# Turning the rows of h for the gates: two 16-bit planes through the DMA crossbar in place of TensorE

## The chip, the cores and the metric

The kernel runs on one core of one Trainium2 chip. The metric is the device time of one execution in microseconds. The engines are named as the profile names them: PE (TensorE's matmuls), PEld (its weight loads), DVE (VectorE), ACT (ScalarE), POOL (GpSimd) and SP (SyncE, which issues every DMA of this kernel on one queue).

## The reference

Two layers over 512 tokens of width 1024. A layer mixes tokens (layer 0 by a neighbourhood attention, layer 1 by a latent attention), adds the result to its input, and then adds a gated embedding. The part that matters here is what stands behind the mixer:

```python
for i in range(DEPTH):
    xn = rmsnorm(x, norm_g[i])
    ...
    h = x + y
    gate = jax.nn.sigmoid(rmsnorm(h, ple_norm[i]) @ ple_w_gate[i])
    x = h + gate * (p[i] @ ple_w_proj[i])
return rmsnorm(x, final_norm)
```

All arrays are 32-bit floats. `y` is the gated output of the mixer times `w_out`.

## The kernel before, in words

A matrix product in full precision is made of three products in a reduced 32-bit format: each operand is split into a high part (ScalarE copies it into that format) and a low part (what is left, by VectorE or GpSimd), and high x high, low x high and high x low are summed in PSUM. So each weight that arrives from memory as `wraw` is split into `whi` (line 77, ScalarE) and `wlo` (line 78, GpSimd), with three buffers of `wraw`; the load of a weight waits until GpSimd has freed the buffer of three loads before.

A layer's second part runs in two stages, for 4 blocks of 128 tokens (t) and 2 halves of 512 columns (n).

- `out_proj` (line 375) multiplies the mixer's output by `w_out`, 24 matmuls for each of the 8 results, and adds each to the rows of the residual in SBUF (`r`, line 387). After each result it calls `turn_h` (line 789).
- `turn_h` multiplies the 128 x 512 piece by the norm's gain (`hg`, line 792, VectorE), turns it into columns, four blocks of 128 x 128, and splits it into the high and the low part of `hnT` (lines 84 and 86, ScalarE and VectorE). `hnT[t]` has 8 column blocks of the high part and 8 of the low; half n fills four of each. A piece is one (t, n); a layer has eight. With n = 1 it also sums the squares of the rows.
- `gate_phase` (line 425) multiplies `hnT[t]` by the gate's weights, again 24 matmuls for each of 8 results (`ps_mm`, two PSUM buffers). A result's matmuls go by weight chunk c = 0 to 3; chunks 0 and 1 use the half n = 0 of `hnT[t]`, chunks 2 and 3 the half n = 1. Then come the sigmoid (line 440, ScalarE), the product with the embedding's projection (line 441) and the add (line 443). In layer 0 the finished rows are normed, turned (`x1n`) and feed the next layer; in layer 1 they are normed and stored.

Turning is done by `transposes` (line 119): four TensorE transposes against an identity into one PSUM tile, `ps_T`, from which both splits read. The same helper turns other rows too, which the change doesn't touch.

Tiles come from pools that hand out buffers in turn: `hg` has three, `ps_T` three, and the pool `zp` (tag "z") eight of 128 x 512, which hold the mixer's gates z and are free by the time of `out_proj`. The order of the instructions on each engine is fixed when the kernel is built, by a scheduler; on the chip each engine takes its instructions in that order, and SyncE's DMAs are issued in the order of its queue.

Of the kernel before, what the change touches and what calls it, by code (L numbers as in the profile page):

```python
# [12 lines left out]

F32 = mybir.dt.float32
F32R = mybir.dt.float32r
AF = mybir.ActivationFunctionType
ALU = mybir.AluOpType
AX = mybir.AxisListType
PSUM = bass.MemoryType.PSUM
P = 128  # L20
S = 512
# [18 lines left out]
class Trunk:  # L40
# [19 lines left out]
    def bigtile(self, name):  # L60
        return self.big.tile([P, 4, S], F32R, name=name, tag="big")

# [5 lines left out]
    def load_w(self, ap, n, extra=False, parts=1, rest=None):  # L68
        nc = self.nc
        pool = self.wx if extra else self.wp  # L70
        raw = self.wp.tile([P, 1024], F32, name="wraw", tag="wraw", bufs=3)
        hi = pool.tile([P, n if extra else 1024], F32R, name="whi", tag="whi", bufs=self.wxn if extra else 3)
        lo = pool.tile([P, n if extra else 1024], F32R, name="wlo", tag="wlo", bufs=self.wxn if extra else 3)
        w = n // parts
        for c in [slice(i * w, (i + 1) * w) for i in range(parts)]:
            nc.sync.dma_start(raw[:, c], ap[:, c])
            nc.scalar.activation(hi[:, c], raw[:, c], AF.Copy)  # L77
            (rest or nc.gpsimd).tensor_tensor(out=lo[:, c], in0=raw[:, c], in1=hi[:, c].bitcast(F32), op=ALU.subtract)  # L78
# [3 lines left out]
    def split(self, hi, lo, src, scale=1.0):  # L82
        nc = self.nc
        self.last_copy = nc.scalar.activation(hi, src, AF.Copy, scale=scale)  # L84
        if scale == 1.0:
# [15 lines left out]
    def inv_rms(self, scratch, src, n):  # L101
        nc = self.nc
        ss = self.small.tile([P, 1], F32, name="ss", tag="ss")
        rs = self.small.tile([P, 1], F32, name="rs", tag="rs")
        nc.scalar.activation(scratch, src, AF.Square, accum_out=ss)
        nc.vector.tensor_scalar(ss, ss, 1.0 / n, EPS, op0=ALU.mult, op1=ALU.add)  # L106
# [19 lines left out]
    def rows_to_cols(self, xn, dst):  # L126

        for g in range(2):
            t = self.transposes([xn[:, (4 * g + i) * P:(4 * g + i + 1) * P] for i in range(4)])
            hi, lo = dst(g)  # L130
            self.split(hi, lo, t.rearrange("p (a b) -> p a b", a=4))


    @staticmethod
    def terms(w, xT, ks):
# [12 lines left out]
    def z_phase(self, wap, xT, js, after=None, R=None, ws=None):  # L148
# [5 lines left out]
        def finish(j, ps):  # L154
            z = zs[j] = self.zp.tile([P, S], F32, name="z", tag="z")
            with self.tc.issue_after(after) if after is not None else nullcontext():
                if R is None:
                    nc.scalar.activation(z, ps, AF.Silu)
                else:
                    nc.vector.tensor_tensor(out=z, in0=ps, in1=R, op=ALU.mult)  # L160
                    nc.scalar.activation(z, z, AF.Silu)

# [23 lines left out]
    def half_of(self, u, O, e):  # L186
        main, rest = (slice(0, 64), slice(64, 128))[::1 - 2 * e]
        self.nc.scalar.activation(u[main], O[rest], AF.Copy)  # L188
        self.nc.vector.tensor_tensor(out=u[main], in0=O[main], in1=u[main], op=ALU.add)  # L189
# [18 lines left out]
    def na_heads(self, pool, xT, zs, oT):  # L208
# [5 lines left out]
        def project(j):  # L214
            if j % 2 == 0:
# [3 lines left out]
                for kt in range(4):  # L219
# [5 lines left out]
                    self.mms(ps[:, :256], t)  # L225
                    vt = pool.tile([P, S], F32R, name="vt", tag="vt", bufs=8)
                    self.v_split(vt, ps[:, :256])
# [3 lines left out]
            self.proj_T(psq, wq, xT)  # L231
            sa = pool.tile([P, S], F32R, name="sa", tag="qs", bufs=4)
            sb = pool.tile([P, S], F32R, name="sb", tag="qs", bufs=4)
            nc.scalar.activation(sa[0:64], psq[0:64], AF.Copy, scale=0.125)
# [482 lines left out]
    def run(self):  # L717
        tc, nc, a = self.tc, self.nc, self.a
# [6 lines left out]
        with tc.tile_pool(name="pre", bufs=4, reuse_waits="tile") as pool:  # L725
            warm = pool.tile([P, S], F32R, name="warm", bufs=1)
            nc.vector.memset(warm.bitcast(F32), 1.0)
            ps = self.psum("T")
# [33 lines left out]
            turned = self.transposes([ss[:, t:t + 1].to_broadcast([P, P]) for t in range(NT)])  # L762
# [14 lines left out]
        for layer in range(2):  # L777
            with tc.tile_pool(name=f"out{layer}", bufs=4, reuse_waits="tile") as pool:
# [10 lines left out]
                def turn_h(t, n):  # L789

                    hg = pool.tile([P, S], F32, name="hg", tag="hg", bufs=3)
                    nc.vector.tensor_tensor(out=hg, in0=res[t][:, n * S:(n + 1) * S],
                                            in1=gp[:, n * S:(n + 1) * S], op=ALU.mult)
                    if n == 0:
                        hnT[t] = self.big.tile([P, 2 * KD, P], F32R, name="hnT", tag="big")
                    ps = self.transposes([hg[:, i * P:(i + 1) * P] for i in range(4)])
                    self.split(hnT[t][:, 4 * n:4 * n + 4, :], hnT[t][:, KD + 4 * n:KD + 4 * n + 4, :],
                               ps.rearrange("p (a b) -> p a b", a=4))
                    if n == 1:
                        sq = pool.tile([P, D], F32, name="sq", tag="xn", bufs=2)  # L800
                        rh[t] = self.inv_rms(sq, res[t], D)

                self.out_proj(a["na_o"] if layer == 0 else a["mla_o"], oT, res, turn_h, last)
                if layer == 0:
                    x1T = ([self.bigtile(f"x1h{g}") for g in range(2)], [self.bigtile(f"x1l{g}") for g in range(2)])
# [143 lines left out]
```

## Time and profile before

| | |
|---|---|
| runs of the kernel | 672.23, 672.34, 673.18 us (median 672.34) |
| the profiled execution, first to last instruction (span) | 670.9 us |
| TensorE matmul busy | 659.2 us (98%) |
| VectorE, ScalarE, GpSimd busy | 367.9 (55%), 408.2 (61%), 396.2 us (59%) |
| granted TensorE clock, mean | 0.998 |

The profiled execution's own time is its span and what lies around it, which the profile doesn't show; the span is 1.4 us under the median of the runs. A row of a timeline gives start and length in us, the engine, the line, the operation, what it writes and reads, the shape and a count; in brackets the idle time before it and what ended that. A row of the chain of work gives start, length, engine, what is written, line and count. A row of groups gives the count, and then busy time in us and mean ns of one. `SPq` rows are DMAs being issued.

### The profile page before, as it was taken

How to read it: one execution, taken by the hardware profiler on the slowest of the kernel's cores; microseconds unless marked ns; L12 is line 12 of the kernel's file. 1: busy time of each engine (PE TensorE's matmuls, PEld its weight loads, DVE VectorE, ACT ScalarE, POOL GpSimd, SP SyncE). 2: the span in 40 equal slices, each digit the busy share in tenths (PEclk: the TensorE clock that was granted, in tenths of full speed). 3: DMA queues.
4: the chain of work that ended last, by engine and by line, in shares of the span. 5: the costliest groups of instructions: out<-in, count | busy, mean ns of one | idle time of the engine just before them, and what ended most of it. 6: DMA issues, size and time to landing. Idle time of an engine off the chain costs nothing.

```text
span 670.9 us, 10168 instructions
## 1 busy us (share of the span) xinstructions
PE 659.2 (98%) x3560; PEld 565.9 (84%) x3560; DVE 367.9 (55%) x826; ACT 408.2 (61%) x815; POOL 396.2 (59%) x323
## 2 busy tenths in 40 slices
PE   8999999999999999999999999999999999999995
PEld 6888898988988888888899887888888878888885
DVE  6371555747656614444525603888988875155233
ACT  6763766657757662643433635898979887436423
POOL 0395546656565665943044636786959786858411
PEclk9999999999999999999999999999999999999999
DMA  8944214222232137534243345020211221854022
GB/s 279 376 137 145 99 45 138 88 95 86 67 118 96 62 117 277 189 102 138 94 112 105 107 107 152 24 75 24 68 29 63 65 96 64 299 217 156 33 79 94
DMA packets 31954, 79.11 MB, mean 118 GB/s; under 512 B 4128, under 2 KB 8992, under 8 KB 31904
## 3 DMA queue, kind: packets, MB, share of 16 engines
q1 hardware_dynamic: 31904, 78.47, 35.2%
q8 instruction: 28, 0.46, 0.3%
q14 instruction: 22, 0.18, 0.1%
HBM read 66.92 MB, written 8.39 MB: 112 GB/s over the span
## 4 chain that ended last, share of the span: by engine, by line
PE 88%; ACT 4%; DVE 2%; DMA 2%; POOL 2%; issue 1%; SPq 1%; POOLq 0%; DVEq 0%; ACTq 0%
PE ps_mm L97 49%; PE ps_S L97 11%; PE ps_mm L511 6%; PE ps_T L123 5%; PE ps_O L621 4%; PE ps_T L97 3%; PE ps_O L97 3%; PE ps_O L361 2%; PE ps_mm L168 2%; PE ps_T L349 1%; DMA qe<-rl 1%; PE ps_S L314 1%; PE ps_S L313 1%; POOL ex L606 1%; DMA xT<-xT 1%
## 5 line engine op out<-in xcount | busy, mean ns | idle before, releaser
L78 POOL TENSOR_TENSOR wlo<-wraw,whi 128x1024 fp32r<-128x1024 f32 (+5 forms) x108 | 212.2, 1983 | 93.4 <-ACT whi L77 66.9
L77 ACT ACTIVATE whi<-wraw 128x1024 fp32r<-128x1024 f32 (+5 forms) x108 | 93.2, 886 | 69.0 <-issue 18.0
L606 POOL TENSOR_TENSOR ex<-ex,rc 128x512 f32<-128x512 f32 x64 | 66.2, 1044 | 31.4 <-DVE rc L605 23.1
L97 PE MATMUL ps_mm<-whi,hnT 128*128 128x512 f32 (+1 forms) x272 | 70.2, 378 | 0.0
L97 PEld LDWEIGHTS ps_mm<-whi,hnT 128*128 128x128 f32 x272 | 49.3, 188 | 9.2
L336 POOL TENSOR_TENSOR ex<-ex,rc 128x128 f32<-128x128 f32 (+1 forms) x64 | 34.3, 560 | 38.0 <-DVE rc L332 36.4
L604 ACT ACTIVATE ex<-ps_S,mx 128x512 f32<-128x512 f32 x64 | 44.0, 688 | 12.4 <-DVE mx L602 11.3
L602 DVE TENSOR_REDUCE mx<-ps_S 128x1 f32<-128x512 f32 x64 | 43.8, 684 | 9.8 <-PE ps_S L97 8.9
L86 DVE TENSOR_TENSOR pt_lo<-ps_T,pt_hi 128x512 fp32r<-128x512 f32 x64 | 43.3, 682 | 7.5 <-ACT pt_hi L84 7.1
L331 ACT ACTIVATE ex<-ex,mx 128x128 f32<-128x128 f32 (+1 forms) x64 | 30.2, 473 | 21.8 <-DVE mx L327 21.5
L97 PE MATMUL ps_mm<-xh,whi 128*128 128x512 f32 x152 | 41.0, 400 | 0.1
L84 ACT ACTIVATE pt_hi<-ps_T 128x512 fp32r<-128x512 f32 x64 | 37.8, 595 | 5.2 <-PE ps_T L123 4.9
L97 PE MATMUL ps_mm<-wlo,hnT 128*128 128x512 f32 (+1 forms) x136 | 40.5, 378 | 0.0
L97 PE MATMUL ps_mm<-xh,wlo 128*128 128x512 f32 x152 | 39.2, 392 | 0.0
L97 PE MATMUL ps_mm<-xl,whi 128*128 128x512 f32 x152 | 38.7, 392 | 0.0
L123 PE MATMUL ps_T<-ident,ex 128*128 128x128 f32 x256 | 38.3, 272 | 0.0
L123 PEld LDWEIGHTS ps_T<-ident,ex 128*128 128x128 f32 x256 | 31.5, 140 | 7.6 <-POOL ex L606 0.2
L189 DVE TENSOR_TENSOR u<-ps_O,u 64x512 f32<-64x512 f32 x32 | 22.0, 686 | 24.3 <-ACT u L188 23.8
L97 PEld LDWEIGHTS ps_mm<-xl,whi 128*128 128x128 f32 x152 | 28.1, 188 | 5.7
L107 POOL TENSOR_TENSOR rs<-ss,half 128x1 f32<-128x1 f32 x20 | 12.6, 637 | 34.3 <-DVE ss L106 34.2
L97 PEld LDWEIGHTS ps_mm<-xh,wlo 128*128 128x128 f32 x152 | 28.1, 188 | 5.5
L441 DVE TENSOR_TENSOR sg<-pe,sg 128x512 f32<-128x512 f32 (+1 forms) x17 | 12.4, 728 | 36.1 <-ACT sg L440 36.1
(339 smaller groups left out, 1666.8 us busy)
## 6 DMA issues: line engine op xcount, KB each, us to landing
wraw<-na_qk SPq DMA_DIRECT2D x16, 512.0 KB, 3.4
wraw<-gate SPq DMA_DIRECT2D x16, 512.0 KB, 3.3
pe<-pe SPq DMA_DIRECT2D x24, 256.0 KB, 7.3
wraw<-na_v SPq DMA_DIRECT2D x8, 512.0 KB, 3.4
wraw<-na_o SPq DMA_DIRECT2D x8, 512.0 KB, 3.6
wraw<-mla_z SPq DMA_DIRECT2D x8, 512.0 KB, 3.7
wraw<-mla_o SPq DMA_DIRECT2D x8, 512.0 KB, 3.7
wraw<-na_z SPq DMA_DIRECT2D x6, 512.0 KB, 5.9
```

The lines of the kernel that those rows point to most:

```text
L77: nc.scalar.activation(hi[:, c], raw[:, c], AF.Copy)
L78: (rest or nc.gpsimd).tensor_tensor(out=lo[:, c], in0=raw[:, c], in1=hi[:, c].bitcast(F32), op=ALU.subtract)
L84: self.last_copy = nc.scalar.activation(hi, src, AF.Copy, scale=scale)
L86: nc.vector.tensor_tensor(out=lo, in0=src, in1=hi.bitcast(F32), op=ALU.subtract)
L97: last = self.last_mm = nc.tensor.matmul(out, l, r, start=i == 0, stop=i == n - 1)
L123: self.last_mm = self.nc.tensor.transpose(t[:, i * P:(i + 1) * P], b, self.ident)
L331: self.last_exp = nc.scalar.activation(e, e, AF.Exp, bias=mx[:, qt:qt + 1], accum_out=sm[:, qt:qt + 1])
L336: nc.gpsimd.tensor_tensor(out=e, in0=e, in1=rc[:, qt:qt + 1].to_broadcast([P, e.shape[1]]), op=ALU.mult)
L511: self.last_mm = nc.tensor.matmul(PS[key], *terms[i], start=i == 0, stop=i == len(terms) - 1)
L602: nc.vector.reduce_max(mx, sp, axis=AX.X, negate=True)
L604: nc.scalar.activation(ex, sp, AF.Exp, bias=mx, accum_out=sm)
L606: nc.gpsimd.tensor_tensor(out=ex, in0=ex, in1=rc.to_broadcast([P, S]), op=ALU.mult)
```

## The change

The line that turns a piece in `turn_h` calls a new helper, `turned`, in place of `transposes`. The piece `hg` is seen as words of 16 bits: plane 0 has the lower word of each element, plane 1 the upper. Two VectorE copies put the planes side by side into `pl` (128 x 2 x 512 words of 16 bits). One DMA transpose, issued on SyncE's queue, turns the eight blocks of 128 x 128 words into `tp`. Two VectorE copies weave the planes back into a 32-bit tile `tw`. The two splits then read `tw` in SBUF, where they read `ps_T` in PSUM. All three tiles come from the pool `zp`. No value changes.

```diff
+U16 = mybir.dt.uint16
...
+    def turned(self, src):
+
+        nc = self.nc
+        pl = self.zp.tile([P, 2, S], U16, name="pl", tag="z")
+        words = src.bitcast(U16).rearrange("p (c s) -> p s c", s=2)
+        for s in range(2):
+            nc.vector.tensor_copy(pl[:, s, :], words[:, s, :])
+        tp = self.zp.tile([P, 2, S], U16, name="tp", tag="z")
+        nc.sync.dma_start_transpose(tp.rearrange("p s (c t) -> p (s c) t", c=4), pl.rearrange("p s c -> p (s c)"))
+        out = self.zp.tile([P, S], F32, name="tw", tag="z")
+        words = out.bitcast(U16).rearrange("p (c s) -> p s c", s=2)
+        for s in range(2):
+            nc.vector.tensor_copy(words[:, s, :], tp[:, s, :])
+        return out
...
-                    ps = self.transposes([hg[:, i * P:(i + 1) * P] for i in range(4)])
+                    ps = self.turned(hg)
                     self.split(hnT[t][:, 4 * n:4 * n + 4, :], hnT[t][:, KD + 4 * n:KD + 4 * n + 4, :],
                                ps.rearrange("p (a b) -> p a b", a=4))
```

The helper moves the lines behind it by 16 (`hg` is written at line 808 after, at 792 before).

Three places of the order show what the scheduler makes of it, all in layer 0. VectorE before, from the second `hg` of the layer on (`r_2742` to `r_2748` are the residual rows of token blocks 0 to 3, the four `hg` are the pieces of n = 0 of those blocks):

```order
L792 TENSOR_TENSOR hg_2840<-r_2744,gp_2750 128x512
L792 TENSOR_TENSOR hg_2876<-r_2746,gp_2750 128x512
L792 TENSOR_TENSOR hg_2912<-r_2748,gp_2750 128x512
L86 TENSOR_TENSOR hnT_2806<-ps_T_2807,hnT_2806 128x512
L86 TENSOR_TENSOR hnT_2842<-ps_T_2843,hnT_2842 128x512
L86 TENSOR_TENSOR hnT_2878<-ps_T_2879,hnT_2878 128x512
L86 TENSOR_TENSOR hnT_2914<-ps_T_2915,hnT_2914 128x512
L387 TENSOR_TENSOR r_2742<-ps_T_2946,r_2742 128x512
```

The four products stand together, then the four splits. VectorE after, from the same place (a `COPY` of `pl` writes the planes, one of `tw` weaves them back, x2 for two copies):

```order
L808 TENSOR_TENSOR hg_2843<-r_2744,gp_2750 128x512
L141 COPY pl_2807<-hg_2804 128x512 x2
L808 TENSOR_TENSOR hg_2882<-r_2746,gp_2750 128x512
L808 TENSOR_TENSOR hg_2921<-r_2748,gp_2750 128x512
L147 COPY tw_2812<-tp_2810 128x512 x2
L141 COPY pl_2846<-hg_2843 128x512 x2
L87 TENSOR_TENSOR hnT_2806<-tw_2812,hnT_2806 128x512
L147 COPY tw_2851<-tp_2849 128x512 x2
L141 COPY pl_2885<-hg_2882 128x512 x2
L403 TENSOR_TENSOR r_2742<-ps_T_2958,r_2742 128x512
L87 TENSOR_TENSOR hnT_2845<-tw_2851,hnT_2845 128x512
L403 TENSOR_TENSOR r_2744<-ps_O_3002,r_2744 128x512
```

The copies into `pl` of a piece stand behind the copies out of `tp` of the piece before, for all eight pieces of the layer, and in layer 1 likewise; the split of a piece stands behind the copies into `pl` of the next.

SyncE after, from the first gate weight on (before, the eight loads of gate weights stand in one row without anything between them):

```order
L77 DMA wraw_3138<-gate 128x1024
L143 DMA_TRANSPOSE tp_2810<-pl_2807 128x8x128
L77 DMA wraw_3144<-gate 128x1024
L77 DMA wraw_3150<-gate 128x1024
L143 DMA_TRANSPOSE tp_2849<-pl_2846 128x8x128
L77 DMA wraw_3156<-gate 128x1024
L77 DMA wraw_3286<-gate 128x1024
L143 DMA_TRANSPOSE tp_2888<-pl_2885 128x8x128
L77 DMA wraw_3292<-gate 128x1024
L77 DMA wraw_3298<-gate 128x1024
L143 DMA_TRANSPOSE tp_2927<-pl_2924 128x8x128
L77 DMA wraw_3304<-gate 128x1024
```

The transposes of the first four pieces stand among the eight loads of gate weights; that of the fifth follows the last of them.

TensorE after, the end of the output projection and the first gate matmuls of layer 0 (`hnT_2806`, `hnT_2845` and `hnT_2884` belong to token blocks 0, 1 and 2; `whi_3139` to `whi_3157` are the four chunks of the first half of the gate's columns):

```order
L98 MATMUL ps_mm_3090<-wlo_2954,oh1_481 128x512 x2
L98 MATMUL ps_mm_3164<-whi_3139,hnT_2806 128x512 x4
L98 MATMUL ps_mm_3164<-wlo_3140,hnT_2806 128x512 x2
L98 MATMUL ps_mm_3164<-whi_3145,hnT_2806 128x512 x4
L98 MATMUL ps_mm_3164<-wlo_3146,hnT_2806 128x512 x2
L98 MATMUL ps_mm_3195<-whi_3139,hnT_2845 128x512 x4
L98 MATMUL ps_mm_3195<-wlo_3140,hnT_2845 128x512 x2
L98 MATMUL ps_mm_3195<-whi_3145,hnT_2845 128x512 x4
L98 MATMUL ps_mm_3195<-wlo_3146,hnT_2845 128x512 x2
L98 MATMUL ps_mm_3164<-whi_3151,hnT_2806 128x512 x4
```

No transposes of `hg` are left among the matmuls. The first 24 gate matmuls take the halves n = 0 of blocks 0 and 1; the half n = 1 of block 0 is first needed behind them, then the first half of block 2, the second halves of blocks 1 and 2, and block 3.

## The prediction

> **What bounds the kernel now.** I read the page first, for the share of each engine and for the chain that ended last; then that chain in order of time around the two places where rows of h are turned; then the timelines of VectorE, GpSimd and SyncE there; last the costs of the operations by form. From the page:
>
> ```profile
> span 670.9 us, 10168 instructions
> PE 659.2 (98%) x3560; PEld 565.9 (84%) x3560; DVE 367.9 (55%) x826; ACT 408.2 (61%) x815; POOL 396.2 (59%) x323
> PE 88%; ACT 4%; DVE 2%; DMA 2%; POOL 2%; issue 1%; SPq 1%; POOLq 0%; DVEq 0%; ACTq 0%
> ```
>
> TensorE is busy for 98% of the span and makes 88% of the chain. So an instruction taken off TensorE is worth its time on it, and a wait put onto TensorE costs its full length. The stage that the change touches, busy time by engine, layer 0 (output projection, then gates) and layer 1:
>
> ```profile
> 259.00:284.00 25.00, 25.00 (x122) 20.77 (x121) 14.18 (x20) 12.80 (x17) 17.39 (x9) 1.00 0.57 190
> 284.00:330.00 46.00, 46.00 (x219) 38.31 (x218) 22.00 (x32) 20.14 (x31) 16.60 (x12) 1.00 0.35 115
> 590.00:619.00 29.00, 29.00 (x144) 24.15 (x142) 16.08 (x24) 16.04 (x22) 20.66 (x11) 1.00 0.47 160
> 619.00:663.00 44.00, 44.00 (x219) 37.37 (x218) 16.43 (x31) 16.64 (x31) 13.68 (x11) 1.00 0.18 65
> ```
>
> The columns are the stretch, its length, then PE, PEld, DVE, ACT and POOL busy. TensorE has no gap in any of the four; VectorE and ScalarE are busy about half the time.
>
> **What is removed.** The chain in order of time, layer 0:
>
> ```profile
> 283.71 0.88 PE ps_T L123 x8
> 284.58 1.62 PE ps_mm L97 x7
> 286.20 0.44 PE ps_T L123 x4
> 286.64 3.46 PE ps_mm L97 x15
> 290.10 0.44 PE ps_T L123 x4
> 290.53 32.44 PE ps_mm L97 x143
> 322.98 0.87 PE ps_T L123 x8
> ```
>
> A group of four transposes costs the chain 0.44 us, and there are 16 groups (4 row blocks, 2 halves, 2 layers): 16 x 0.44 = 7.0 us of TensorE go. That is the whole gain. From 290.53 on a matmul costs 32.44 / 143 = 0.227 us.
>
> **What is added, per piece of 512 columns.** Four VectorE copies (two planes out, two back) and one crossbar transpose of 256 KB on SyncE's queue. In number, 64 copies and 16 transposes. VectorE has the time for the copies on average; the point is where they stand. The order in the section on the change shows VectorE's queue as: copies into pl of piece 0, copies out of tp of piece 0 (these wait for the transpose), and only then the copies into pl of piece 1. The engine takes its queue in order, so the transpose of piece 1 can't be issued before that of piece 0 has landed, and so on through the eight pieces of a layer: one transpose is in flight at a time. Behind the waiting copy stand the adds of the residual (r), the other hg products and the split of the piece before. A round trip has the length
>
> p = two copies + (transpose, issue to landing) + two copies + hand-overs.
>
> Before, nothing of this stood in a row: TensorE turned a piece as soon as hg was there.
>
> The rows for the price of a round trip. Copies between SBUF tiles, and the hg product beside them:
>
> ```profile
> L243 DVE CAST s<-sb x8: 209/218/270, 65.3 to 207.4; 128x128 fp32r<-128x128 f32 x8
> L833 DVE TENSOR_SCALAR r<-r,rs x1: 345/345/345, 666.8 to 666.8; 128x256 f32<-128x256 f32 x1
> L792 DVE TENSOR_TENSOR hg<-r,gp x16: 678/692/2882, 260.4 to 620.1; 128x512 f32<-128x512 f32 x16
> ```
>
> A copy of 512 words of 16 bits is not in the trace. Its bounds are 0.345 us (256 words of 32 bits, the same bytes) and 0.69 us (hg, 512 results). The slope of the first two rows, 0.345 - 0.218 = 0.127 us for 128 columns, gives 0.345 + 2 x 0.127 = 0.60 us, which I take; four make 2.4 us. On top of the upper end comes a wait: hg's largest time, 2.882 us, fell while GpSimd made a low part of a weight (2.40 us, below). One such wait per round trip is the upper end: 4 x 0.69 + 2.4 = 5.2 us. The lower end is 4 x 0.345 = 1.4 us.
>
> Landings in the trace (KB each, median us):
>
> ```profile
> ko<-slab_h SPq DMA_DIRECT2D x2, 128.0 KB, 2.3
> wraw<-mla_kv SPq DMA_DIRECT2D x8, 256.0 KB, 2.9
> out<-r SPq DMA_DIRECT2D x8, 256.0 KB, 2.2
> gn<-final_norm SPq DMA_DIRECT2D x1, 512.0 KB, 9.3
> ```
>
> No DMA of before turns anything. 2.3 us is a plain move from SBUF to SBUF of half the bytes: the lower end. 9.3 us is the longest landing in the table, of a DMA that reads one row 128 times over and was issued behind others: the upper end. A transpose gathers each destination row from 128 partitions in words of 2 bytes, which is as far from moving rows as that one; but nothing will be queued ahead of it. I take the middle of the plain 256 KB (2.9) and 9.3: 6.1 us. The Trainium skill says otherwise in two places, which disagree with each other. Advanced Engine Details and Errata, section X-Bar Transpose (TRN2), has transposing DMAs as fast as regular ones; by it the landing would be near the plain 2.9 us, and the loss almost nothing. VectorE: DVE Perf Modes, section The three transpose paths, has one 128x128 block of 16-bit words at 1309 ns on the crossbar against 390 ns on TensorE, and advises TensorE where PSUM will do; eight blocks would be 10.5 us, an estimate, and the loss about double mine. No row of before decides between them.
>
> Hand-overs cost little: ScalarE's sigmoid below ends at 294.89 and VectorE's product starts at 294.93. I put 0.1 us for a round trip. So p = 2.4 + 6.1 + 0.1 = 8.6 us, with ends 1.4 + 2.3 + 0.1 = 3.8 and 5.2 + 9.3 + 0.1 = 14.6.
>
> **What eight round trips do to the path.** Starts and ends, from the timelines of VectorE, GpSimd, ScalarE and TensorE:
>
> ```profile
> 260.39 0.68 DVE L792 TENSOR_TENSOR hg<-r,gp 128x512 f32<-128x512 f32 x1
> 262.19 2.31 DVE L792 TENSOR_TENSOR hg<-r,gp 128x512 f32<-128x512 f32 x2
> 260.95 2.40 POOL L78 TENSOR_TENSOR wlo<-wraw,whi 128x1024 fp32r<-128x1024 f32 x1 [3.60 <-ACT whi L77]
> 592.56 3.48 DVE L792 TENSOR_TENSOR hg<-r,gp 128x512 f32<-128x512 f32 x2
> 294.20 0.69 ACT L440 ACTIVATE sg<-ps_mm,rs 128x512 f32<-128x512 f32 x1
> 294.93 0.69 DVE L441 TENSOR_TENSOR sg<-pe,sg 128x512 f32<-128x512 f32 x1 [3.03 <-ACT sg L440]
> 295.65 0.69 DVE L443 TENSOR_TENSOR r<-r,sg 128x512 f32<-128x512 f32 x1
> 663.06 0.40 PE L97 MATMUL ps_mm<-wlo,hnT 128*128 128x256 f32 x2
> ```
>
> The first copies into pl stand behind the second hg of the layer. In layer 0 the two hg at 262.19 end at 264.50, so the first of them at about 264.5 - 0.7 = 263.8. In layer 1 it runs 592.56 to about 593.2, ahead of GpSimd. Then come 8p. Behind the last copies out of tp stand a product, an add and the split of the last piece, 3 x 0.69 = 2.1 us. Only then can TensorE take the second half of row block 3; the order of TensorE keeps behind that point 12 matmuls of it and the 96 of the other half of the columns. 108 x 0.227 = 24.5 us. In layer 0 two pairs of groups of x1n, 2 x 0.87 = 1.7 us, lie among them.
>
> Layer 0, end of the gate matmuls after: 263.8 + 8p + 2.1 + 24.5 + 1.7 = 292.1 + 8p. Before: at 290.53 + 32.44 = 322.97, 7 + 15 + 143 = 165 of 192 matmuls are done; 27 x 0.227 + 1.7 more give 330.8. Difference 8p - 38.7. Layer 1: after 593.2 + 8p + 2.1 + 24.5 = 619.8 + 8p; before 663.5. Difference 8p - 43.7. Together 16p - 82.4, the 7.0 us of removed transposes included, since the path after holds none of them. It breaks even at p = 5.15 us. With p = 8.6: +55.2 us from the round trips alone.
>
> A gap on TensorE costs a little more than its length. The warm-up matmuls at the start, and the stretches behind the last matmul (the clock is the third number from the end):
>
> ```profile
> 1.48 3.78 PE L730 MATMUL ps_T<-warm 128*128 128x512 f32 x8 [1.48 <-DVE warm L727]
> 663.50:667.00 3.50, 0.00 (x0) 0.00 (x0) 1.72 (x6) 1.58 (x4) 1.16 (x2) 1.00 0.32 119
> 667.00:670.80 3.80, 0.00 (x0) 0.00 (x0) 0.15 (x1) 0.12 (x1) 0.00 (x0) 0.73 0.37 138
> ```
>
> The clock falls once TensorE has been idle for over 3.5 us, and eight matmuls from rest take 3.78 us in place of 8 x 0.227 = 1.8: a loss of 2.0 us. Only the gap ahead of the last 108 matmuls counts, since the earlier ones are inside the wait. With p = 8.6 that gap is 8.8 us between the splits of the last two pieces less a burst of 24 matmuls, 3.4 us, or 1.4 if the burst was itself slow: at the limit. I count 2.0 us for the two layers, with 0 and 4.0 as ends. So +57.2 us.
>
> All else hides: between two pieces TensorE has at most 24 matmuls (5.4 us) that don't wait for the next piece, less than p, so it stands idle, and whatever ScalarE (its split now reads SBUF) and VectorE add lies in that idle time. The work behind the gates keeps its length and moves by the sum; so does the end of the kernel. What covers the change today is the 23 to 26 us between the first hg and the first gate matmul; it holds four to five round trips at break-even and not eight at 8.6.
>
> SyncE's queue adds a floor. The transposes stand among the loads of gate weights, two to a transpose:
>
> ```profile
> 257.37 24.79 SPq L76 DMA_DIRECT2D wraw<-gate  x8
> ```
>
> These eight loads wait for buffers that GpSimd frees, and the fourth and fifth transposes stand behind the seventh and eighth of them, so not before about 280 even if a transpose cost nothing. Piece 3 is due there at 263.8 + 3 x 8.6 = 289.6, so at my p the loads wait for the transposes, not the other way.
>
> The median of the runs is 672.34 us, 1.4 above the span; I leave those 1.4 as they are and forecast 672.3 + 57.2 = 729.5 us.
>
> **The rivals.** First, a crossbar that is slower: landing at the upper end with one wait for GpSimd per round trip, p = 14.6, 16 x 14.6 - 82.4 + 4.0 = +155.2 us, 827.5 us. For it: 2-byte words from 128 partitions. Against it: the plain rows between 2.2 and 2.9. The 1309 ns of the Trainium skill (VectorE: DVE Perf Modes) would put it at p of about 13, an estimate. Second, the crossbar lands like a plain DMA, 2.9 us, p = 2.4 + 2.9 + 0.1 = 5.4: 16 x 5.4 - 82.4 = +4.0 us, 676.3 us, the gaps being too short to slow the clock. The Trainium skill's "as fast as regular" (Advanced Engine Details and Errata) is this case. The GpSimd waits and the floor on SyncE speak against so little. Third, on the other side: with p under 5.15 us eight round trips end before TensorE has done the output projection and the first halves, the chain hides whole, and the removed transposes are won: -7.0 us, 665.3 us. It needs a landing under 2.65 us at my price of copies, and 2.3 us for half the bytes speaks against that. Fourth, the transpose is not done by the crossbar but word by word, as 131,072 elements: far over the first rival, no bound from a row.
>
> **How the numbers follow.** Chances: forecast (p from 6 to 11) 0.60, slow crossbar 0.23, plain landing 0.09, hidden 0.04, word by word 0.02, and 0.02 for p at break-even. The range reaches from the second rival to the upper bound: 676 to 828 us; the hidden case, break-even and the part of the slow cases beyond 828 are left out. The likeliest case alone has 672.3 + (16 x 6 - 82.4) = 686 to 672.3 + (16 x 11 - 82.4) + 4.0 = 770. Over 0.2% of the time, 1.3 us and about what a measurement of this kernel tells from no change: faster 0.04, same 0.03, slower 0.93.
>
> **What the changed profile would show.** Right: TensorE idle in two stretches only, between the output projection and the second halves of hnT, waiting for the split of hnT; one transpose in flight at a time, eight per layer at a spacing of about 8.6 us; VectorE's largest wait is for the DMA of tp at the copy into tw; the granted clock falls in the longest gaps and stands at 1.00 elsewhere. Wrong: transposes overlapping each other, a spacing under 5 us with TensorE full, a wait for gate weights in place of hnT, or lost time outside these two stages.

## The result and the profile after

Before 672.5 us (median of 4 runs), after 702.6 us (4 runs, 700.3 to 703.7): the ratio is 1.0434, with a 95% interval of 1.0408 to 1.046. The change costs 30.0 us where 57.2 were forecast; the time lies in the forecast's range of 676 to 828 us, far below its middle. The profiled execution has a span of 701.3 us, 30.4 above that of before; the accounts below are made against it.

The page of the kernel after, the same rows as were read of before, and the row of the granted clock:

```profile
span 701.3 us, 10121 instructions
PE 663.9 (95%) x3496; PEld 564.8 (81%) x3496; DVE 417.4 (60%) x890; ACT 408.4 (58%) x815; POOL 398.1 (57%) x323
PEclk9999999999999999869999999999999999998999
PE 77%; DVE 10%; DMA 5%; ACT 4%; issue 1%; POOL 1%; SPq 1%; POOLq 0%; DVEq 0%; ACTq 0%
```

TensorE has 64 matmuls fewer, as it should, and is still busy 4.7 us longer. Its share of the chain falls from 88% to 77%; VectorE and the DMA take 15%. The stretches of busy time by engine, layer 0 and layer 1 (length, then PE, PEld, DVE, ACT and POOL busy, then the granted clock, the third number from the end):

```profile
284.00:301.00 17.00, 8.37 (x26) 6.05 (x27) 13.84 (x24) 6.99 (x10) 13.06 (x8) 0.74 0.51 139
301.00:318.00 17.00, 14.88 (x49) 11.41 (x49) 8.14 (x17) 4.33 (x6) 0.00 (x0) 0.76 0.47 88
635.00:656.00 21.00, 11.51 (x37) 7.93 (x36) 17.29 (x22) 7.85 (x12) 11.27 (x8) 0.84 0.34 75
656.00:669.00 13.00, 11.31 (x49) 9.05 (x50) 8.37 (x17) 5.85 (x11) 1.44 (x2) 1.00 0.39 75
```

TensorE is half idle in the first and the third, and its clock is down. How the time comes about is read from SyncE's queue, where the first and the last transpose of each layer stand:

```profile
267.13 1.34 SPq L143 DMA_TRANSPOSE tp<-pl  x1
311.10 1.24 SPq L143 DMA_TRANSPOSE tp<-pl  x1
613.13 1.28 SPq L143 DMA_TRANSPOSE tp<-pl  x1
662.80 1.24 SPq L143 DMA_TRANSPOSE tp<-pl  x1
```

Eight transposes a layer, seven spacings: (311.10 - 267.13) / 7 = 6.28 us in layer 0 and (662.80 - 613.13) / 7 = 7.10 us in layer 1. That is the round trip p, forecast at 8.6. One trip in the chain of work, layer 0:

```profile
270.50 0.71 DVE tw L147 x2
271.21 0.64 DVE pl L141 x2
271.86 0.02 issue
271.88 3.06 DMA tp<-pl
274.94 0.02 issue
274.96 3.80 DVE tw L147 x2
278.76 0.63 DVE pl L141 x2
```

Copies out of one piece, copies into the next, transpose, copies out: one transpose in flight, as the order said. A transpose lands in 3.06 us; two copies take 0.64 to 0.71 us when nothing is in the way and 3.80 us when something is. The copies by tile, min/median/max in ns:

```profile
L141 DVE COPY pl<-hg x32: 401/414/2628, 264.1 to 662.3; 128x512 uint16<-128x512 uint16 x32
L147 DVE COPY tw<-tp x32: 432/450/2650, 270.4 to 666.3; 128x512 uint16<-128x512 uint16 x32
```

The groups of VectorE's work on h by form (count, busy us, mean ns, then the idle time ahead of them and what ended it):

```profile
L141 DVE COPY pl<-hg 128x512 uint16<-128x512 uint16 x32 | 21.7, 719 | 0.0
L147 DVE COPY tw<-tp 128x512 uint16<-128x512 uint16 x32 | 25.1, 836 | 20.7 <-DMA tp<-pl 20.7
L808 DVE TENSOR_TENSOR hg<-r,gp 128x512 f32<-128x512 f32 x16 | 23.1, 1457 | 0.0
```

At their medians the 64 copies would take 32 x 0.414 + 32 x 0.450 = 27.6 us; they take 46.8. The 19.2 us between are long copies, and where one stands, GpSimd makes a low part of a weight. Layer 1, VectorE and GpSimd at the same time:

```profile
640.26 5.04 DVE L141 COPY pl<-hg 128x512 uint16<-128x512 uint16 x2
645.23 0.68 DVE L403 TENSOR_TENSOR r<-ps_mm,r 128x512 f32<-128x512 f32 x1
640.00 5.02 POOL L79 TENSOR_TENSOR wlo<-wraw,whi 128x1024 fp32r<-128x1024 f32 x2
```

Two copies start 0.3 us behind GpSimd's first low part and end 0.3 us behind its second, at 645.3; the add of the residual stands behind them. The Trainium skill has a rule for this (SBUF — State Buffer, section SBUF: two separate sides): VectorE and GpSimd share one pair of ports as an exclusive lock, and the loser waits for the whole instruction. The rows agree: the longest copies, 2.63 and 2.65 us, are as long as a low part of 2.4 us and a little.

TensorE's timeline where it waits (idle time and what ended it in brackets):

```profile
284.81 1.69 PE L98 MATMUL ps_mm<-whi,hnT 128*128 128x512 f32 x4 [2.70 <-DVE ss L107]
290.35 1.17 PE L98 MATMUL ps_mm<-whi,hnT 128*128 128x512 f32 x4 [0.97 <-DVE r L403]
300.20 2.07 PE L98 MATMUL ps_mm<-whi,hnT 128*128 128x512 f32 x4 [6.85 <-ACT hnT L85]
307.80 1.19 PE L98 MATMUL ps_mm<-whi,hnT 128*128 128x512 f32 x4 [2.12 <-ACT sg L456]
646.05 2.04 PE L98 MATMUL ps_mm<-whi,hnT 128*128 128x512 f32 x4 [6.98 <-DVE r L403]
```

The group of these matmuls on the page, with the idle time ahead of them in both layers:

```profile
L98 PE MATMUL ps_mm<-whi,hnT 128*128 128x512 f32 (+1 forms) x272 | 76.7, 405 | 23.8 <-DVE r L403 8.9
```

And a row of the chain, the matmuls behind the wait of 6.85 us:

```profile
300.20 5.50 PE ps_mm L98 x12
```

All idle time in the two stages is 23.8 us: 8.9 end with an add of the residual (L403), 8.9 with ScalarE's split of hnT (L85), 3.4 with a sigmoid (L456) and 2.7 with `ss` (L107). Then the clock: at 300.20, after 6.85 us of idling, 12 matmuls take 5.50 us in place of 12 x 0.227 = 2.7. Over the four stretches above TensorE was busy 8.37 + 14.88 + 11.51 + 11.31 = 46.1 us with 26 + 49 + 37 + 49 = 161 matmuls, which at 0.227 take 36.5: about 9.5 us are lost to the lower clock. The account of the span: 23.8 + 9.5 - 7.0 (transposes gone) = 26.3 of 30.4 us.

Another part lies outside the two stages, in layer 1's attention. A wait on TensorE's timeline, and TensorE's stretch behind it (length, then PE busy, the granted clock, the DMA share and GB/s):

```profile
505.99 0.50 PE L98 MATMUL ps_S<-ke,qe 96*128 96x512 f32 x1 [1.78 <-DMA qe<-rl]
506.00:510.00 4.00, 4.00 (x14) 0.64 0.04 9
```

This wait for a DMA of 1.78 us is followed by a clock of 0.64. From the matmul behind the DMA wait of 0.81 us (415.34 before, 431.30 after) to the one behind the wait of about 1.1 us for ScalarE (542.84 before, 562.01 after), the lag behind the kernel before grows from 15.96 to 19.17 us: 3.2 us, 1.8 of waiting and 1.4 of slower matmuls. That makes 29.5 of 30.4 us; 0.9 us is not traced. Whether the change brings this wait about is open: the experiments below show it at 0.6 to 2.1 us or not at all.

### The profile page after: what moved, and what is told of

The parts are those of the page before. It is cut to its first block, busy times and chain, and to the rows that moved or that the text cites. A ratio compares the mean times of both kernels' runs of the same rounds, so it can differ in the third digit from the quotient of the medians.

```text
span 701.3 us, 10121 instructions
## 1 busy us (share of the span) xinstructions
PE 663.9 (95%) x3496; PEld 564.8 (81%) x3496; DVE 417.4 (60%) x890; ACT 408.4 (58%) x815; POOL 398.1 (57%) x323
## 4 chain that ended last, share of the span: by engine, by line
PE 77%; DVE 10%; DMA 5%; ACT 4%; issue 1%; POOL 1%; SPq 1%; POOLq 0%; DVEq 0%; ACTq 0%
PE ps_mm L98 42%; PE ps_S L98 10%; PE ps_mm L527 6%; PE ps_T L124 4%; PE ps_O L637 4%; DMA tp<-pl 3%; DVE tw L147 3%; DVE hg L808 2%; DVE pl L141 2%; PE ps_O L377 2%; PE ps_T L98 2%; PE ps_mm L184 2%; PE ps_T L365 1%; DMA qe<-rl 1%; PE ps_S L330 1%
## 5 line engine op out<-in xcount | busy, mean ns | idle before, releaser
L98 PE MATMUL ps_mm<-whi,hnT 128*128 128x512 f32 (+1 forms) x272 | 76.7, 405 | 23.8 <-DVE r L403 8.9
L98 PEld LDWEIGHTS ps_mm<-whi,hnT 128*128 128x128 f32 x272 | 52.4, 202 | 38.4 <-issue 11.8
L98 PE MATMUL ps_mm<-wlo,hnT 128*128 128x512 f32 (+1 forms) x136 | 42.7, 397 | 0.0
L85 ACT ACTIVATE pt_hi<-ps_T 128x512 fp32r<-128x512 f32 x64 | 37.7, 595 | 7.0 <-PE ps_T L124 6.7
L147 DVE COPY tw<-tp 128x512 uint16<-128x512 uint16 x32 | 25.1, 836 | 20.7 <-DMA tp<-pl 20.7
L205 DVE TENSOR_TENSOR u<-ps_O,u 64x512 f32<-64x512 f32 x32 | 22.0, 686 | 24.3 <-ACT u L204 23.8
L85 ACT ACTIVATE hnT<-tw 128x512 fp32r<-128x512 f32 x16 | 10.1, 630 | 41.9 <-DVE tw L147 41.9
```

Source lines behind the costliest of these rows:

```text
L98: last = self.last_mm = nc.tensor.matmul(out, l, r, start=i == 0, stop=i == n - 1)
L147: nc.vector.tensor_copy(words[:, s, :], tp[:, s, :])
```

## The experiments

The theory after the result: the loss has two causes that work on each other. The order of VectorE allows one transpose in flight (order), and each trip is drawn out by copies and products that wait for GpSimd (port). Rivals: the crossbar or SyncE's queue is the limit, or every piece has its price wherever it stands. Each kernel was timed beside the kernel before; ratios are to that.

**Without GpSimd's low parts, and its control.** The edit, made to the kernel after and to the kernel before:

```diff
...
-            (rest or nc.gpsimd).tensor_tensor(out=lo[:, c], ...)
-        return hi, lo
+            if low:
+                (rest or nc.gpsimd).tensor_tensor(out=lo[:, c], ...)
+        return hi, lo if low else hi
...
-            ws = [self.load_w(a["gate"][layer, n, c], 1024, extra=...)
+            ws = [self.load_w(a["gate"][layer, n, c], 1024, low=False, extra=...)
```

> The changed kernel, but GpSimd makes no low parts of the gate weights; the high part is used again in their place, so TensorE does the same number of matmuls, and the output is not the reference's. It is to be read against the kernel before with the same edit. Theory of GpSimd waits (half of a round trip above its landing is VectorE's copies waiting for GpSimd's 2.4 us low parts): without them a round trip is 3.06 (landing) + 0.71 + 0.64 (copies) + 0.05 = 4.5 us, 16 x 4.5 - 82.4 is under zero, the chain hides, and this kernel is 7 us faster to 5 us slower than its control. Rival, landing and order alone (the waits only fill time in which VectorE waits for the transpose anyway): the round trip stays at 6 to 7 us and the loss at 25 to 30 us over the control.

> The control: the kernel before without GpSimd's low parts of the gate weights (the high part is used twice; the output is not the reference's). TensorE is full there with or without them, so both theories expect 670 to 674 us, within 2 us of the kernel before.

Measured: 684.6 us (ratio 1.0169, 1.0136 to 1.0202) against 672.9 for the control (1.0002, 0.9992 to 1.0011). So 11.6 us of loss stay of 30.0, between the two theories: neither 7 faster to 5 slower nor 25 to 30. The copies without low parts of the gate weights, by tile:

```profile
L143 DVE COPY pl<-hg x32: 404/417/2629, 262.8 to 641.8; 128x512 uint16<-128x512 uint16 x32
L149 DVE COPY tw<-tp x32: 435/454/475, 271.2 to 646.8; 128x512 uint16<-128x512 uint16 x32
```

The copies out of tp by form, with the idle time ahead of them:

```profile
L149 DVE COPY tw<-tp 128x512 uint16<-128x512 uint16 x32 | 12.7, 454 | 28.4 <-DMA tp<-pl 28.2
```

The longest copy out of tp is 0.475 us, where it was 2.65: the waits of these copies were GpSimd's. The first copies into pl of each layer still reach 2.63 us; GpSimd then makes the last low parts of the output projection's weights, which this edit leaves. But VectorE now waits 28.2 us for transposes where it waited 20.7, since the order is the same. The round trip falls to 5.3 us (first and last transpose at 268.00 and 305.17 us in layer 0, at 606.44 and 643.36 in layer 1), not to the 4.5 of the expectation. (The edit also frees the weights' buffers earlier, so the loads come earlier; the experiment with the transposes on ScalarE's queue bears on what that is worth.)

**Two or three transposes in flight.** The copies out of tp and the split are written two pieces later; everything else is the same, in number and size:

```diff
-                    ps = self.turned(hg)
-                    self.split(hnT[t]..., ps...)
+                    late.append((t, n, self.turned(hg)))
+                    while len(late) > (2 if (t, n) != (NT - 1, 1) else 0):
+                        weave(*late.pop(0))
```

> The changed kernel with the copies out of tp and the split of a piece written two pieces later, so that two or three transposes can be in flight; the same instructions in number and size. Theory of the order (one transpose in flight): VectorE's 20.7 us of waiting for tp mostly go, the waits for GpSimd stay, and the loss of 30 us falls to between 0 and 15 us: 672 to 688 us. Rival, GpSimd waits alone: VectorE's work with its waits is what takes the time, and at most 8 us come back, 694 to 703. Rival, the crossbar or SyncE's queue is the limit: no change, 700 to 705, and landings grow when transposes overlap.

Measured: 696.1 us, ratio 1.0344 (1.0328 to 1.036): 6.5 us come back, which is what the rival of the port foretold; the 672 to 688 us of the order theory are missed. VectorE's groups there:

```profile
L151 DVE COPY tw<-tp 128x512 uint16<-128x512 uint16 x32 | 19.1, 650 | 0.5 <-DMA tp<-pl 0.5
L141 DVE COPY pl<-hg 128x512 uint16<-128x512 uint16 x32 | 26.7, 877 | 0.0
L87 DVE TENSOR_TENSOR hnT<-tw,hnT 128x512 fp32r<-128x512 f32 x16 | 17.5, 1096 | 2.5 <-ACT hnT L85 2.1
```

The wait for transposes is gone, 0.5 us of 20.7, as the order theory said. The time went into the other wait: the copies into pl rose from 719 to 877 ns on the mean and the split from 684 to 1096. Taking one cause away leaves VectorE to meet the other more often. TensorE's waits in the two stages come to 18.3 us, of which 15.3 end with an add of the residual that stands on VectorE behind these copies; the longest:

```profile
295.77 2.08 PE L98 MATMUL ps_mm<-whi,hnT 128*128 128x512 f32 x4 [5.50 <-DVE r L407]
```

**Both at once.** The two edits in one kernel.

> Both edits of the first two experiments in one: copies out of tp and splits written two pieces later, and no low parts of the gate weights by GpSimd (the high part is used twice; the output is not the reference's). The control is the kernel before with the same weights, 672.9 us. If the loss of 30 us is the order (one transpose in flight) and the waits for GpSimd, and nothing else, then nothing is left of it and the 7 us of transposes on TensorE show: 664 to 674 us. If something third costs (the transposes slow each other, SyncE's queue holds the gate weights back, the copies as such), 10 us or more of loss stay, above 682.

Measured: 673.1 us, ratio 1.0004 (0.9989 to 1.0019), against 672.9 for the control. Nothing of the loss against the kernel before is left. Order and port together are the whole of it: taking away the port alone gives back 18.4 us, the order alone 6.5, both 29.9. Where the low parts are gone in both kernels, the order is worth 11.5 us (684.6 to 673.1). TensorE's timeline, the longest waits that remain in the two layers:

```profile
283.95 2.98 PE L100 MATMUL ps_mm<-whi,hnT 128*128 128x512 f32 x12 [1.68 <-DVE r L409]
287.75 3.03 PE L100 MATMUL ps_mm<-whi,hnT 128*128 128x512 f32 x12 [0.81 <-DVE ss L109]
...
630.24 10.06 PE L100 MATMUL ps_mm<-whi,hnT 128*128 128x512 f32 x43 [0.74 <-ACT sg L462]
```

The landings of its transposes in us:

```profile
DMA to landing us min/median/max: 3.1/4.7/6.9
```

The 7.0 us that the removed transposes should win don't show: six waits of 0.2 to 1.7 us, 4.7 in all, eat most of them. And the landing is longer, 4.7 us in the median. The first three transposes of a layer are issued 1.4 to 1.6 us apart here, beside loads that come earlier; in the deferred kernel with its low parts they are 2.4 to 2.7 us apart, and the median landing is 3.2. Which of the two lengthens the landing isn't separated.

**A second transpose in each trip**, `tq` from `tp`, with the copies reading `tq`.

```diff
+        tq = self.zp.tile([P, 2, S], U16, name="tq", tag="z")
+        nc.sync.dma_start_transpose(tq.rearrange(...), tp.rearrange("p s c -> p (s c)"))
...
-            nc.vector.tensor_copy(words[:, s, :], tp[:, s, :])
+            nc.vector.tensor_copy(words[:, s, :], tq[:, s, :])
```

> The changed kernel with a second DMA transpose behind the first in each piece (tp is turned again into another tile, from which the copies read), so a round trip holds two landings of 3.1 us; the blocks are turned twice, so the output is not the reference's. Theory of the order: each of the 16 round trips grows by up to 3.1 us, less what VectorE's other work now hides in the longer wait: 20 to 50 us over the changed kernel, 722 to 753 us. If the landing is not on the path (GpSimd waits or TensorE's clock make the loss): under 15 us more, below 718.

Measured: 738.6 us, ratio 1.0982 (1.095 to 1.1014), 36.0 us over the kernel after: 36.0 / 16 = 2.25 us for each added landing of 3.1. Of the 36.0, 4.7 us are not waiting: TensorE is busy 668.6 us there against 663.9, at a lower clock. VectorE's wait for transposes went from 20.7 to 60.6 us:

```profile
L149 DVE COPY tw<-tq 128x512 uint16<-128x512 uint16 x32 | 19.3, 657 | 61.4 <-DMA tq<-tp 60.6 <-POOL rs L108 0.8
```

**Half of the pieces.** The crossbar for n = 0 alone, then for n = 1 alone:

```diff
-                    ps = self.turned(hg)
+                    ps = self.turned(hg) if n == 0 else self.transposes([...])
```

> The crossbar turns only the pieces of n = 0 (four a layer); those of n = 1 are turned by TensorE as before. Theory of the order, with the slack of 23 to 26 us between the first product hg and the first gate matmul: four round trips of 6 to 7 us take 25 to 28 us and lie nearly all in that slack; TensorE is rid of 3.5 us of transposes and waits 0 to 4 us in each layer: 668 to 677 us, far under half of the loss of eight. Rival, a price per piece (copies, DMA, waits cost the same wherever the piece stands): half of the 30 us, 685 to 690.

> The crossbar turns only the pieces of n = 1 (four a layer); those of n = 0 are turned by TensorE. Theory of the order: the first transpose of a layer can start only with the fifth product, about 15 us later than in the changed kernel, and TensorE needs the first of these pieces behind 24 gate matmuls (5.4 us), the others each 24 matmuls later; the first round trip is about at the limit, the others take 6 to 7 us against 5.4 of matmuls: 2 to 6 us of waiting a layer less 1.8 us of transposes, 673 to 682 us. Rival, a price per piece: 685 to 690.

Measured: 681.7 us (1.0129, 1.0091 to 1.0167) and 681.2 us (1.0128, 1.0099 to 1.0157). Four pieces cost 9 us, eight cost 30: no price per piece. For n = 1 the time lies in the range of the order's theory, near its upper end. For n = 0 it is 5 us above the range, and the trace shows why. TensorE waits for the rows of the other half, in layer 0:

```profile
284.90 1.26 PE L124 MATMUL ps_T<-ident,hg 128*128 128x128 f32 x8 [2.50 <-DVE hg L808]
290.50 0.66 PE L124 MATMUL ps_T<-ident,hg 128*128 128x128 f32 x4 [1.69 <-DVE hg L808]
```

Of 8.9 us of waits in the two layers, 5.8 are such waits for hg. The products hg of n = 1, which TensorE itself turns, stand on VectorE behind copies that wait. The slack of 23 to 26 us covers the pieces, not what is queued behind them.

**The deferred kernel with its transposes on ScalarE's queue.**

```diff
-        nc.sync.dma_start_transpose(...)
+        nc.scalar.dma_start_transpose(...)
```

> The deferred kernel of the second experiment with its transposes issued on ScalarE's queue, so that the loads of gate weights on SyncE's queue stand behind no transpose. If the 24 us that the deferred kernel still loses come from gate weights held back in SyncE's queue (GpSimd was idle for 9.9 us there before the third low part), 8 us or more come back: under 688 us. If they are VectorE's waits for GpSimd, the earlier low parts only move these waits: 690 to 700.

Measured: 693.2 us, ratio 1.0298 (1.0279 to 1.0317), 2.9 us less than on SyncE's queue. By this run the weights held back in SyncE's queue are worth that much and no more, net of the 1.25 us of ScalarE's queue that each transpose now takes. The waits for GpSimd moved from the copies into pl to those out of tp, 858 ns on the mean.

**The deferred kernel with the copies on ScalarE.**

```diff
-            nc.vector.tensor_copy(pl[:, s, :], words[:, s, :])
+            nc.scalar.copy(pl[:, s, :], words[:, s, :])
...
-            nc.vector.tensor_copy(words[:, s, :], tp[:, s, :])
+            nc.scalar.copy(words[:, s, :], tp[:, s, :])
```

> The deferred kernel with all four copies of a piece on ScalarE instead of VectorE; nothing is left out. If the waits for GpSimd are VectorE's alone, ScalarE's copies have none (about 0.6 us each, no 2.6 us among them), and of the 24 us that the deferred kernel lost most comes back, since only hg and the split are left to wait on VectorE: 670 to 682 us. If any engine's copy in SBUF waits for GpSimd, or if the copies as work are the cost: 690 or more.

Measured: 690.0 us, ratio 1.0245 (1.0229 to 1.0261). The premise is borne out, the time isn't. The copies by tile:

```profile
L141 ACT COPY pl<-hg x32: 600/615/632, 261.5 to 638.5; 128x512 uint16<-128x512 uint16 x32
L151 ACT COPY tw<-tp x32: 747/762/781, 268.3 to 643.6; 128x512 uint16<-128x512 uint16 x32
```

VectorE's split by form:

```profile
L87 DVE TENSOR_TENSOR hnT<-tw,hnT 128x512 fp32r<-128x512 f32 x16 | 20.6, 1304 | 30.1 <-ACT hnT L85 30.1
```

TensorE's longest wait in layer 0, from its timeline:

```profile
296.17 2.08 PE L98 MATMUL ps_mm<-whi,hnT 128*128 128x512 f32 x4 [8.12 <-ACT hnT L85]
```

None of 64 copies on ScalarE waited (max 0.632 and 0.781 us), while VectorE's split did: it now reads two tiles of SBUF, at 1304 ns on the mean (2483 at most), and in the kernel before, reading `ps_T`, it never took more than 0.693 us, though GpSimd made low parts at the same time (from 267.60 to 281.81 us without a pause):

```profile
L86 DVE TENSOR_TENSOR hnT<-ps_T,hnT x16: 676/691/693, 266.6 to 628.0; 128x512 fp32r<-128x512 f32 x16
```

But ScalarE takes its queue in order as VectorE does, with the copies among the high parts of weights and the sums of squares, and TensorE waits 8.12 us for ScalarE's split. The longest wait in layer 1, 5.09 us, is for ScalarE's split too: the bound has moved to ScalarE.

**The deferred kernel with the low parts on VectorE.**

```diff
-            ws = [self.load_w(a["gate"][layer, n, c], 1024, extra=...)
+            ws = [self.load_w(a["gate"][layer, n, c], 1024, rest=nc.vector, extra=...)
```

> The deferred kernel with the low parts of the gate weights made by VectorE instead of GpSimd; nothing is left out. The waits for GpSimd go, and VectorE gets 8 low parts of about 1.3 us a layer in their place, 10 us of work. If the waits (2.4 us at a time, while VectorE stands) are the cost, 672 to 684 us. If VectorE's time in the stage is what is short, whoever takes it, the 10 us a layer replace the waits: 690 to 700.

Measured: 684.1 us, ratio 1.0171 (1.0156 to 1.0187), just past the upper end of the first range. VectorE has 19.3 us of low parts more to do, its busy time still falls from 421.8 to 409.0 us, and the kernel is 12.0 us faster than the deferred one: its standing still cost more than this work. 11 us of loss stay, and this run doesn't show whether the added work is their cause.

**Half of the pieces, deferred, copies on ScalarE.** The experiment of n = 0 with the two edits that take VectorE's waits away from the copies:

```diff
+                    if n == 0:
+                        late.append((t, n, self.turned(hg)))
+                    while len(late) > (2 if n == 0 else 0):
+                        weave(*late.pop(0))
+                    if n == 1:
+                        ps = self.transposes([...])
```

> The crossbar turns the pieces of n = 0 only, deferred by two pieces, with the copies on ScalarE; TensorE turns those of n = 1. Nothing is left out. By the order and the waits for GpSimd, both taken away here, the four pieces lie in the slack of 23 to 26 us ahead of the gates, and TensorE is rid of 8 of 16 groups of transposes, 3.5 us: 668 to 673 us, the one version that could end below the kernel before. If four pieces cost TensorE 2 us or more a layer in another way (hg held up on VectorE, splits late on ScalarE), 674 to 680.

Measured: 672.7 us, ratio 1.0002 (0.9987 to 1.0018): no change. The 9 us that four pieces cost are gone, by hiding them; the 3.5 us of transposes that TensorE is spared don't show. In the profiled execution one wait for a sigmoid on ScalarE, 2.36 us in layer 0, takes most of them; ScalarE had stood idle for 3.05 us shortly before, until the load of a gate weight had landed. VectorE's products hg and its splits still wait for GpSimd (up to 2.89 us), without a gap on TensorE that ends with them. It is the best version with the crossbar found here, and it doesn't beat the kernel before.

**Low parts in quarters**, in the kernel after and its order:

```diff
...
+            v = w // cut
+            for d in [slice(c.start + i * v, c.start + (i + 1) * v) for i in range(cut)]:
-            (rest or nc.gpsimd).tensor_tensor(out=lo[:, c], in0=raw[:, c], ...)
+                (rest or nc.gpsimd).tensor_tensor(out=lo[:, d], in0=raw[:, d], ...)
...
-            ws = [self.load_w(a["gate"][layer, n, c], 1024, extra=...)
+            ws = [self.load_w(a["gate"][layer, n, c], 1024, cut=4, extra=...)
```

> The changed kernel, in its own order, with GpSimd's low part of each gate weight made in four pieces of 256 columns instead of one of 1024; nothing is left out. If a waiting VectorE instruction has to wait until the GpSimd instruction that runs has ended, the longest copy falls from 2.6 us to about 0.4 + 0.6 = 1.0 us, most of the 18 us that the waits cost come back, and the time is 686 to 696 us. If GpSimd keeps VectorE out through a row of its instructions (the next one starts ahead of VectorE), copies stay near 2.6 us and the time between 699 and 705.

Measured: 696.1 us, ratio 1.0344 (1.0327 to 1.0361), at the edge of the first range. The copies out of tp by tile:

```profile
L149 DVE COPY tw<-tp x32: 439/809/1072, 271.8 to 657.4; 128x512 uint16<-128x512 uint16 x32
```

GpSimd's quarters by form:

```profile
L81 POOL TENSOR_TENSOR wlo<-wraw,whi 128x256 fp32r<-128x256 f32 x64 | 56.5, 915 | 4.9 <-ACT whi L78 4.9
```

The longest copy out of tp falls from 2.65 to 1.07 us, so a wait lasts until the running instruction of GpSimd ends. (The longest copy into pl stays at 2.63 us: it is the first of a layer, beside a low part of the output projection's weights, which are not cut.) But the median copy rises from 0.450 to 0.809, and four quarters take 4 x 0.915 = 3.66 us where one low part took 2.45: the two engines now make each other wait more often. A third of what the low parts cost comes back (6.5 of 18.4 us).

## Why the prediction came out as it did

**The mechanism was right.** The sign, the place and the chain are those of the forecast: what TensorE newly idles lies between the output projection and the gates but for 1.8 us at 506 us, one transpose is in flight, the clock is down there and, but for the 4 us behind that wait, at 1.00 elsewhere. That a landing stands on the path is shown by the doubled transposes (+36.0 us). That the order costs is shown by the deferral, 11.5 us where GpSimd makes no low parts of the gate weights, and order and port together leave nothing of the loss.

**The landing was mis-sized.** The step that was off is "I take the middle of the plain 256 KB (2.9) and 9.3: 6.1 us". The landing was 3.1 us in the median, at the plain end. That a transpose gathers words of 2 bytes from 128 partitions was no reason for the 9.3 us of a broadcast of one row. Of the two places in the Trainium skill, Advanced Engine Details and Errata (X-Bar Transpose (TRN2)), as fast as regular DMAs, agrees with the trace. The estimate of 10.5 us, worked out from the 1309 ns for one block of the Trainium skill's VectorE: DVE Perf Modes (The three transpose paths), does not, since eight blocks landed in 3.1 us, 0.39 each.

**The copies were about right for a wrong reason.** 0.60 us each was forecast; the medians are 0.41 and 0.45, with starts 0.32 to 0.36 apart (0.64 and 0.71 for two). The wait for GpSimd, which I had put at the upper end alone, is the rule: 19.2 us in 16 trips, 1.2 a trip in the copies, and hg waits beside them (1457 ns on the mean against 693 in the median, 12 us in 16 of them, of which the kernel before had 6.4 already, at no cost there). The copies' busy time is 46.8 / 16 = 2.9 us a trip against the forecast 2.4. Without waits a trip would be 3.06 + 0.71 + 0.64 + 0.05 = 4.5 us, below the break-even of 5.15; the kernel without low parts of the gate weights came to 5.3. Measured it was 6.28 and 7.10, on the mean 6.69 instead of 8.6. That 6.69 still lies in the likeliest band (6 to 11) is in part luck: the forecast's own copies with the true landing give 2.4 + 3.1 + 0.1 = 5.6 us, below the band, and the waits put it back.

**The sum.** By the formula, 16 x 6.69 - 82.4 = +24.6 us; so the true p takes 30.6 us off the forecast 55.2. The formula doesn't hold the other 5.4 us of the measured 30.0. It misses more without the low parts: 16 x 5.3 - 82.4 = +2.4 us, where 11.6 were measured. Its step "Only then can TensorE take the second half of row block 3" names the eighth piece as the one that decides. In layer 0 the fifth did: TensorE waited 6.85 us for it until 300.20, and ran without a gap from 307.80 on, while the eighth landed only at about 311.10 + 3.1 = 314.2. In layer 1 the longest wait, 6.98 us, ended at 646.05, before the last three transposes were issued. And the gaps ahead of the earlier pieces cost clock as well: "Only the gap ahead of the last 108 matmuls counts" gave 2.0 us, the trace has about 9.5. Its rule "The clock falls once TensorE has been idle for over 3.5 us" doesn't hold: in the kernel after the clock was down behind waits of 1.78, 2.12 and 2.70 us too (0.64 in the 4 us behind the first), while it stayed at 1.00 behind the 2.36 us of the kernel that turns half of the pieces with copies on ScalarE. These runs give no threshold. Two small slips: the 8.8 us between two splits are 8.6 by its own spacing, and the formula reaches the -7.0 us of the hidden chain at p = 75.4 / 16 = 4.7, not at 5.15.

**What TensorE waits for.** The forecast had it wait for the split of hnT. Of 23.8 us, 8.9 end so, and as many with an add of the residual: it frees the PSUM buffer that the next gate result needs, and it stands on VectorE behind the copies (the 6.98 us at 646.05 end with the add at 645.23, which follows the copies that GpSimd held for 5.04 us). In the code the last results of the output projection and the first of the gates share the two buffers of ps_mm. The 2.7 us that the profile puts down to `ss` are probably one more such wait: the gate matmul doesn't read `ss`, and an add of ps_mm stands right ahead of it on VectorE (from 283.99 to 284.67, the matmul starts at 284.81). The text had named these adds as queued behind the waiting copy, and not who waits for them.

**SyncE's queue.** "the loads wait for the transposes, not the other way" held: all sixteen transposes were issued within 0.1 us of the end of their copies, and taking them off that queue gave 2.9 us in the deferred kernel.

**The rivals.** The plain landing was the true one, and its +4.0 us were not: the waits for GpSimd, named against it, made most of the difference. The slow crossbar and the transpose word by word are ruled out by the same landing of 3.1 us. The hidden chain (-7.0) appeared at best as no loss, once both causes were gone.

## What to carry to other kernels

Work that is moved to an engine with time on average is priced by its place in that engine's queue: look at what it waits for there, at whom it makes wait, and at which of its instructions stop for another engine. Two causes in one chain don't add: taking away one of them (18.4 or 6.5 of 30 us) can give far less than both (29.9), so a weak result of one fix doesn't clear its cause. Where one end of a price is a plain row of the same size and the other is a row of another kind, take the plain one until something in the trace speaks against it.

## What the runs showed of the hardware

- A crossbar transpose of 256 KB in words of 16 bits, SBUF to SBUF: landing 3.0 to 4.7 us, median 3.1, and 1.24 us of SyncE's queue to issue it, where the load of a weight takes 0.33. With several in flight beside the loads the median was 4.7 in one kernel and 3.2 in another that issues them farther apart.
- VectorE's copies of 16-bit words with a step of two take 0.32 to 0.36 us for 512, and wait for a running low part of GpSimd (up to 2.65 us in all); ScalarE's copies of the same take 0.615 and 0.762 us and never waited (64 copies, 0.781 us at most). A VectorE split with both inputs in SBUF waits (1304 ns on the mean, 2483 at most), the same with one in PSUM did not (688, 693 at most).
- After 6.85 us without a matmul, 12 matmuls took 5.50 us in place of 2.7, and the mean granted clock of 301 to 318 us was 0.76. After only 1.78 us it was 0.64 over the next 4 us; after 2.36 us in another kernel it was 1.00.
